# Warming matmuls, row sums, rotation copies and the last root in a one-core encoder block

## The chip, the cores and the metric

The kernel runs on one NeuronCore of a Trainium2 chip. The metric is the device time of one execution in microseconds, the median of several runs. Engines are called PE (TensorE matmul), PEld (its weight loads), DVE (VectorE), ACT (ScalarE), POOL (GpSimd) and SP (SyncE, which issues most transfers). PE writes to PSUM; ACT and DVE read it.

## The reference, cut to what matters

One layer over x of 512 rows and 1024 columns, all in float32:

```
h  = RMSNorm(x);  proj = h @ W_in          # q, k, v of differential attention; q, k, v, g of retention; two gates
dq, dk = rope(dq), rope(dk)
A  = differential attention (4 heads);  B = bidirectional retention (4 heads)
m  = sigmoid(gate_a) * (A @ W_upA) + sigmoid(gate_b) * (B @ W_upB)
x  = x + m @ W_o
x  = x + SwiGLU(RMSNorm(x))
y  = RMSNorm_final(x)
```

RMSNorm(x) is x * rsqrt(mean(x*x) + 1e-5) * g, with the mean along a row. rope turns pairs of columns of each head by an angle that depends on the row.

## The kernel before, in words

The work of all engines is written out by generators. Each generator yields the engine and the operands of its next instruction; `Streams.run` (L204) keeps a modelled clock for every engine and always emits the instruction that could start first by that model, with a rank to settle ties. The order of each engine's instructions is thus fixed at build time by modelled costs; on the chip every engine takes its list in order and waits only for data. A float32 matrix product is made of three products of float32r parts (`mm3`, L103): high by high, high by low, low by high. The splitting copies (`copy` on ACT, a subtraction on DVE) feed every product.

**Start.** `warm_gen` (L321) puts WARM = 9 matmuls of a 128x128 matrix of ones (float32, two records each in the trace) ahead of everything. Meanwhile `load_gen` (L335) fetches tiles of x and the first weights half by half; `conv_gen` (L386) splits the weights and `xsplit_gen` (L460) the x tiles, into `h_h` and `h_l`. `main_gen` (L1109) begins with the first four passes, "pfirst": four column tiles i of the projection (dq0, dk0, dq1, dk1), each a sum over eight tiles k of x, in a written order that follows what arrives: (0,0), (1,0), (0,1), (1,1), (2,0) and so on, the whole of tile 3 last. They sit in the PSUM pools "w" (three banks) and "o" (two banks).

**Row sums.** `xsquare_gen` adds up the squares of x, tile by tile. `rstd_gen` (L493) splits the sum, waits for the mark "pfirst" (set when all four passes are emitted), and lets PE sum over partitions: `ssq_b` (two matmuls of 512 columns) and `ssq_c` (four pairs of 4 columns, in a bank of the pool "mm", which has three). `rsqrt` (L480) makes the root: Ln, Exp and Square on ACT, then two `scalar_tensor_tensor` (STT) on DVE. It gives `rb`, with which the rope tables are scaled (`cosr` on DVE, `sinr` on POOL; then the mark "rope" is set), and `rcol`, a column for the values.

**Rotations.** `rope_gen` (L562), spawned for the four tiles after the passes, waits for "rope". Four ACT copies of 32 partitions swap quarters out of PSUM into `sw`; DVE makes `t1` = PSUM times `cosr` and the bank is released; POOL multiplies `sw` by `sinr` and adds it to `t1`; a split follows. `scores_gen` starts when q and k of a head are there. The later rotations (bank "mm") use the same function.

**Values.** `proj_v("dv")` (L1052) follows the passes: two groups of two row tiles, each group 48 matmuls. The second group can start only when two "mm" banks are free, so it waits for the evacuation of the first group's first tile (`v_evac_gen`, L721: ACT writes `dv_h` with the scale `rcol`, DVE writes `dv_l`).

**End.** The last stage adds the down projection to the residual and normalises row tile by row tile. `x2_gen` (L1001) adds PSUM to `x1t`, squares with a row sum (`accum_out`) into columns of `ss`, and multiplies by the gain into `u`. For the last tile, right half, add and square are done in two halves of 256 columns. `final_gen` (L1016) adds the columns of `ss` (a reduce), takes `rsqrt`, scales both halves of `u` (one on DVE, one on ACT for the last tile) and stores them.

Of the kernel before, what the change touches and what calls it, by code (L numbers as in the profile page):

```python
# [13 lines left out]
AF = mybir.ActivationFunctionType  # L14
ALU = mybir.AluOpType
AX = mybir.AxisListType

P = 128
T = 512
D = 1024  # L20
KT = D // P
NT = T // P
# [3 lines left out]
EPS = 1e-5  # L26
# [198 lines left out]
def block_kernel(ctx: ExitStack, tc: tile.TileContext, xT, w_st, w_v, w_g, w_up, w_o, w_f, w_fl,  # L225
# [8 lines left out]
    nc = tc.nc  # L234
# [7 lines left out]
    E = Streams(nc)  # L242
# [8 lines left out]
    done = set()  # L251

    def slot(name, dt=F32):
        return sp.tile([P, T], dt, tag="slot", name=name, bufs=NSLOT)
# [4 lines left out]
    def small(shape, name, dt=F32, bufs=1, tag=None):  # L259
        return cp.tile(shape, dt, tag=tag or name, name=name, bufs=bufs)  # L260

    def psum(tag, name):
        t = yield from E.acquire(tag)
        ps = pp.tile([P, T], F32, tag=tag, name=name, bufs=PS_BUFS[tag])
        E.mark(ps, t)
        return ps

    def split(src, name, after=None):

        h, l = slot(f"{name}_h", F32R), slot(f"{name}_l", F32R)  # L270
        yield from E.copy(h, src)
        yield from E.tt(l, src, h.bitcast(F32), ALU.subtract)
        return h, l

    def have(*names):
        return lambda: all(n in done for n in names)
# [22 lines left out]
            return (w_g if g[0] == "g" else w_db)[int(g[1]), b, u]  # L299
        return w_fl[b] if g == GROUPS - 1 else w_f[g, b, u]  # L300

    WARM = 9


    gcs = small([P, 25], "gcs")
# [6 lines left out]
    ones32 = small([P, P], "ones32")  # L312
# [3 lines left out]
    eps_c = small([P, 1], "eps_c")  # L316
# [4 lines left out]
    def warm_gen():  # L321

        ps = yield from psum("mm", "warm")
        for _ in range(WARM):
            nc.tensor.matmul(ps[:, 0:P], lhsT=ones32, rhs=ones32, start=True, stop=True)
        E.did("pe", 0.43 * WARM, [ps], [])
        E.release("mm", ps)

    xt, hh, hl = {}, {}, {}
# [125 lines left out]
    def drop(w):  # L455
        E.release("HL", w[1])
# [20 lines left out]
                yield from E.tt(acc, acc, sq, ALU.add)  # L477
        done.add("acc")

    def rsqrt(ps, n, name, out):  # L480

        w = ps.shape[-1]
        y0 = slot(f"{name}_y0")[:, :w]
        yield from E.act(out, ps, AF.Ln, scale=1.0 / n, bias=eps_c)
        yield from E.act(y0, out, AF.Exp, scale=-0.5)
        yield from E.act(out, y0, AF.Square, scale=math.sqrt(0.5 / n))
        yield from E.stt(out, ps, n * EPS, out, ALU.add, ALU.mult)
        yield from E.stt(out, out, 1.5, y0, ALU.subtract, ALU.mult, reverse0=True)

    rb, cosr, sinr = slot("rb"), slot("cosr"), slot("sinr")  # L490
# [2 lines left out]
    def rstd_gen():  # L493

        yield have("acc")
        ah, al = yield from split(acc, "accx")
        yield have("pfirst")
        ps = yield from psum("w", "ssq_b")
        yield from E.mm(ps, (ones, ah, True, False), (ones, al, False, True))
        ps2 = yield from psum("mm", "ssq_c")  # L500
        for j in range(NT):
            js = slice(j * P, (j + 1) * P)
            yield from E.mm(ps2[:, 4 * j:4 * j + 4], (ah[:, js], ones[:, 0:4], True, False),
                            (al[:, js], ones[:, 0:4], False, True))
        yield from rsqrt(ps, D, "rb", rb)
        E.release("w", ps)
        done.add("rb")
        yield from E.tt(cosr, cos_raw, rb, ALU.mult)
        yield from E.tt(sinr, sin_raw, rb, ALU.mult, eng="pool")
        done.add("rope")  # L510
        yield from rsqrt(ps2[:, 0:16], D, "rc", rcol)
        E.release("mm", ps2)
        done.add("rcol")
# [48 lines left out]
    def rope_gen(ps, bank, scale, name, key, is_k):  # L562

        yield have("rope")
        sw, t1 = slot(f"{name}_sw"), slot(f"{name}_t1")
        for a, b in ((0, 32), (32, 0), (64, 96), (96, 64)):
            yield from E.act(sw[a:a + 32, :], ps[b:b + 32, :], AF.Copy, scale=scale)
        yield from E.stt(t1, ps, scale, cosr, ALU.mult, ALU.mult)
        E.release(bank, ps)
        yield from E.tt(sw, sw, sinr, ALU.mult, eng="pool")  # L570
        yield from E.tt(t1, t1, sw, ALU.add, eng="pool")
        (ks if is_k else qs)[key] = yield from split(t1, name)

    def norm(po, name, gain=None, gate_tile=None):

        sq = slot(f"{name}_sq")
        yield from E.act(sq, po, AF.Square)
        sh, sl = yield from split(sq, f"{name}_sq")
        yield "pe", [sl]
        pn = yield from psum("w", f"{name}_ssq")  # L580
        yield from E.mm(pn, (ones, sh, True, False), (ones, sl, False, True))
        y = slot(f"{name}_y")
        yield from rsqrt(pn, P, name, y)
        E.release("w", pn)
        if gain is not None:
            yield from E.stt(y, po, gain, y, ALU.mult, ALU.mult)
            E.release("o", po)
        else:
            yield from E.tt(y, po, y, ALU.mult)
            E.release("o", po)  # L590
            yield have("rg")
            yield from E.tt(y, y, rg[gate_tile], ALU.mult, eng="pool")
        return (yield from split(y, f"{name}_o"))
# [407 lines left out]
    def x2_gen(i, hf, ps, ss):  # L1001

        t, u = x1t[i, hf], slot(f"u{i}{hf}")
        n = 2 if hf and i == NT - 1 else 1
        w = T // n
        for c in range(n):
            cs = slice(c * w, (c + 1) * w)
            yield from E.tt(t[:, cs], t[:, cs], ps[:, cs], ALU.add if i < 2 else ALU.subtract)
            sq = slot(f"sq3_{i}{hf}{c}")[:, :w]
            yield from E.act(sq, t[:, cs], AF.Square, accum_out=ss[:, hf + c:hf + c + 1])  # L1010
        yield from E.tt(u, t, gfs[hf], ALU.mult)
        X2[i, hf] = u

    X2 = {}

    def final_gen(i, ss):  # L1016
        yield lambda: (i, 0) in X2 and (i, 1) in X2
        s3, r3 = small([P, 1], f"s3_{i}"), small([P, 1], f"r3_{i}")
        yield from E.reduce(s3, ss, ALU.add)
        yield from rsqrt(s3, D, f"r3_{i}", r3)  # L1020
        a, b = X2[i, 0], X2[i, 1]
        yield from E.ts(b, b, r3, None, ALU.mult)
        yield from E.dma(y[i][:, T:D], b, sbuf_in=True)
        if i < NT - 1:
            yield from E.ts(a, a, r3, None, ALU.mult)
            yield from E.dma(y[i][:, 0:T], a, sbuf_in=True)
        else:
            yield from E.act(a, a, AF.Copy, scale=r3)
            yield from E.dma(y[i][:, 0:T], a, sbuf_in=True, q=nc.scalar)


    def proj_t(name, src, n_k=KT, w=None, off=0, bank="mm"):

        w0 = w or (yield from take())
        ps = yield from psum(bank, name)
        for k in range(n_k):
            cs = slice((off + k) * P, (off + k + 1) * P)
            yield lambda: k in src
            yield from E.mm3(ps, w0[0][:, cs], w0[1][:, cs], *src[k], k == 0, k == n_k - 1)
        if w is None:  # L1040
            drop(w0)
        return ps
# [66 lines left out]
    def main_gen():  # L1109
        ps0 = []  # L1110
# [4 lines left out]
        ws = {}  # L1115
        for i, k in order:
            yield lambda: ("conv", i, k // 4) in done and k in hh
            ws[i] = conv[i]
            cs = slice(k * P, (k + 1) * P)
            yield from E.mm3(ps0[i], ws[i][0][:, cs], ws[i][1][:, cs], hh[k], hl[k], k == 0, k == KT - 1)  # L1120
            if k == KT - 1:
                conv.pop(i)
                used[0] += 1
                drop(ws[i])
        done.add("pfirst")
        E.spawn(rope_gen(ps0[0], "w", 0.125, "dq0", 0, False), 10)
        E.spawn(rope_gen(ps0[1], "w", 1.0, "dk0", 0, True), 10)
        E.spawn(rope_gen(ps0[2], "o", 0.125, "dq1", 1, False), 11)
        E.spawn(rope_gen(ps0[3], "o", 1.0, "dk1", 1, True), 11)
        for h in range(HEADS):  # L1130
# [6 lines left out]
        for name in ORDER:  # L1137
# [4 lines left out]
            ps = yield from proj_t(name, hT)  # L1142
# [7 lines left out]
        for b, src in enumerate((oA, oB)):  # L1150
            for hf in range(2):
                us = []
                for i in range(NT):
                    ps = yield from psum("mm", f"up{hf}{b}{i}")
                    for k in range(HEADS):
# [3 lines left out]
                        cs, ts_ = slice(k % 2 * T, (k % 2 + 1) * T), slice(i * P, (i + 1) * P)  # L1159
# [24 lines left out]
        for n, ks_ in ((0, range(4)), (1, range(4)), (0, range(4, KT)), (1, range(4, KT)),  # L1184
# [4 lines left out]
            for k in ks_:  # L1189
                cs = slice(k * P, (k + 1) * P)  # L1190
# [24 lines left out]
        bank = {}  # L1215
# [30 lines left out]
        for i in range(NT):  # L1246
            ss = small([P, 3 if i == NT - 1 else 2], f"ss3_{i}")
            for hf in range(2):
                for k in range(FT - TAIL, FT):
                    yield from down(i, hf, k, k == FT - 1)  # L1250
                E.spawn(x2_gen(i, hf, pd[i, hf], ss), 10)
            E.spawn(final_gen(i, ss), 10)

    E.spawn(warm_gen(), 0)
    E.spawn(load_gen(), 0)
    E.spawn(conv_gen(), 2)
# [84 lines left out]
```

## Time and profile before

| | us |
|---|---|
| median of three runs | 725.46 (725.22 to 726.31) |
| the profiled execution | 725.72 |
| its span, first to last instruction | 723.5 |
| PE busy | 705.2 |
| DVE busy | 542.3 |
| ACT busy | 493.3 |

A timeline row is: start, duration, engine, line, operation, output <- inputs, shape, count, and in brackets the idle time just ahead and what ended it. A matmul's duration overlaps the next one's, so the pace of PE is read from one start to the next.

### The profile page before, as it was taken

The page shows a single profiled execution, that of the slowest core. Times are in us where ns is not written, and L with a number is a line of the kernel's source. Part 1 is how long each engine was busy: PE and PEld are TensorE (multiplying, and loading weights), DVE is VectorE, ACT ScalarE, POOL GpSimd, SP SyncE. Part 2 cuts the span into 40 slices and gives each one's busy share as a digit, 9 for nine tenths or more (in the row PEclk, how much of TensorE's full clock was granted, in tenths as well). Part 3 has the DMA queues.
Part 4 walks back from the last instruction along what each step waited for, and adds up shares of the span by engine and source line. Part 5 has one row for each costly group of instructions (what it writes and reads, how often), then busy time and mean ns, then how long its engine had stood idle before and what let it go on. Part 6 is the DMA issues. An engine that isn't in the chain of part 4 may idle for free.

```text
span 723.5 us, 9200 instructions
## 1 busy us (share of the span) xinstructions
PE 705.2 (97%) x3284; PEld 568.7 (79%) x3284; DVE 542.3 (75%) x796; ACT 493.3 (68%) x816; POOL 114.5 (16%) x137
## 2 busy tenths in 40 slices
PE   9989999999989999999999999999999999999996
PEld 7867677777758888887888888888888888787884
DVE  6667787869867478887677677667676789989645
ACT  7688897787687667665557876555656578777433
POOL 4360421011015001300000100000010011332000
PEclk9999999999999999999999999999999999999999
DMA  8802110302235628866522857658483887899202
GB/s 327 321 7 74 59 58 31 117 29 88 88 117 132 189 87 255 241 201 189 151 41 88 254 124 192 186 169 214 150 232 115 255 197 161 225 258 276 78 6 110
DMA packets 33661, 110.18 MB, mean 152 GB/s; under 512 B 4016, under 2 KB 4016, under 8 KB 33616
## 3 DMA queue, kind: packets, MB, share of 16 engines
q1 hardware_dynamic: 23328, 78.14, 30.7%
q0 software_dynamic: 10000, 30.94, 21.5%
q8 instruction: 25, 0.41, 0.2%
q10 hardware_dynamic: 288, 0.52, 0.2%
q14 instruction: 20, 0.16, 0.1%
HBM read 102.25 MB, written 2.10 MB: 144 GB/s over the span
## 4 chain that ended last, share of the span: by engine, by line
PE 84%; ACT 7%; DVE 6%; issue 1%; DMA 0%; SPq 0%; ACTq 0%; DVEq 0%
PE fY L91 16%; PE fZ L91 8%; PE wo L91 6%; PE up L91 6%; PE fYd L91 5%; PE fYg L91 5%; PE fX L91 4%; PE pfirst L91 3%; PE rg L91 3%; PE rv L91 3%; PE fZd L91 3%; PE fZg L91 3%; PE fXd L91 2%; PE dv L91 2%; PE fXg L91 2%; PE s L100 1%
## 5 line engine op out<-in xcount | busy, mean ns | idle before, releaser
L91 PE MATMUL fY<-w_h,S 128*128 128x512 f32 (+1 forms) x384 | 117.5, 376 | 0.0
L91 PEld LDWEIGHTS fY<-w_h,S 128*128 128x128 f32 x384 | 70.4, 188 | 12.1
L126 DVE TENSOR_TENSOR w_l<-w_r,w_h 128x1024 fp32r<-128x1024 f32 (+1 forms) x50 | 56.6, 1136 | 30.7 <-ACT w_h L121 30.2
L121 ACT CAST w_h<-w_r 128x1024 fp32r<-128x1024 f32 (+1 forms) x50 | 48.8, 980 | 34.6 <-issue 8.1
L91 PE MATMUL fY<-w_l,S 128*128 128x512 f32 (+1 forms) x192 | 71.4, 372 | 0.0
L91 PE MATMUL fZ<-w_h,S 128*128 128x512 f32 (+1 forms) x192 | 58.6, 377 | 0.0
L91 PE MATMUL fYd<-w_h,S 128*128 128x512 f32 x128 | 41.1, 391 | 0.0
L91 PEld LDWEIGHTS fY<-w_l,S 128*128 128x128 f32 x192 | 36.2, 189 | 5.7
L91 PEld LDWEIGHTS fZ<-w_h,S 128*128 128x128 f32 x192 | 35.3, 188 | 6.1
L91 PE MATMUL fZ<-w_l,S 128*128 128x512 f32 (+1 forms) x96 | 35.7, 371 | 0.0
L91 PE MATMUL fYg<-w_h,S 128*128 128x512 f32 x96 | 31.1, 391 | 0.0
L91 PE MATMUL fX<-w_h,S 128*128 128x512 f32 (+1 forms) x96 | 28.5, 371 | 0.0
L91 PEld LDWEIGHTS fYd<-w_h,S 128*128 128x128 f32 x128 | 24.0, 188 | 4.9
L116 ACT ACTIVATE fg<-fg,r 128x512 f32<-128x512 f32 (+1 forms) x24 | 16.0, 684 | 15.7 <-DVE fg L126 15.7
L91 PE MATMUL wo<-m_h,w_h 128*128 128x512 f32 x64 | 25.4, 397 | 0.0
L91 PE MATMUL wo<-m_l,w_h 128*128 128x512 f32 x64 | 25.1, 393 | 0.3 <-DVE m_l L126 0.2
L91 PE MATMUL wo<-m_h,w_l 128*128 128x512 f32 x64 | 24.9, 390 | 0.0
L91 PE MATMUL fYd<-w_l,S 128*128 128x512 f32 x64 | 24.9, 389 | 0.0
L169 POOL DMA_DIRECT2D x1t<-cd x20 | 18.0, 932 | 43.8 <-ACT cd L116 21.5
L150 DVE TENSOR_REDUCE mx<-s 128x1 f32<-128x512 f32 x32 | 21.2, 681 | 4.5 <-PE s L100 4.4
L116 ACT ACTIVATE e<-s,mx 128x512 f32<-128x512 f32 x32 | 21.9, 687 | 2.1 <-DVE mx L150 1.7
L121 ACT COPY snap_v<-fY 128x512 f32<-128x512 f32 (+1 forms) x24 | 13.2, 550 | 12.0 <-PE fY L91 12.0
(563 smaller groups left out, 2100.4 us busy)
## 6 DMA issues: line engine op xcount, KB each, us to landing
w_r<-w_st SPq DMA_DIRECT2D x12, 512.0 KB, 4.3
x1t<-cd POOLq DMA_DIRECT2D x20, 256.0 KB, 7.0
w_r<-w_v SPq DMA_DIRECT2D x8, 512.0 KB, 5.6
w_r<-w_up SPq DMA_DIRECT2D x8, 512.0 KB, 3.2
w_r<-w_o SPq DMA_DIRECT2D x8, 512.0 KB, 4.3
w_r<-w_d SPq DMA_DIRECT2D x6, 512.0 KB, 5.6
x<-xT SPq DMA_DIRECT2D x8, 256.0 KB, 5.6
w(g_a)_r<-w_g SPq DMA_DIRECT2D x4, 512.0 KB, 3.1
```

Of the source, the lines that this page charges most:

```text
L91: self.nc.tensor.matmul(out, lhsT=lhsT, rhs=rhs, start=start, stop=stop, skip_group_check=more)
L100: self.nc.tensor.matmul(outs[i % 2], lhsT=lhsT, rhs=rhs, start=i < 2, stop=i >= len(ops) - 2)
L116: self.nc.scalar.activation(out, in_, func, **kw)
L121: self.nc.scalar.copy(out=out, in_=in_)
L126: (self.nc.vector if eng == "dve" else self.nc.gpsimd).tensor_tensor(out=out, in0=a, in1=b, op=op)
L150: self.nc.vector.tensor_reduce(out=out, in_=a, axis=AX.X, op=op, **kw)
L169: self.nc.gpsimd.dma_start(out=out, in_=in_, accum_op=ALU.add)
```

## The change

- WARM is 10, and the warming generator adds one more matmul of ones after the mark "p0". That mark is set when the first three products of the passes, (0,0), are emitted; of these the low weight part now comes second and the low x part third.
- The mark "pfirst", on which the row sums wait, is set after (3,1) instead of after all passes.
- In rotations out of the pools "w" and "o" (the first four), the copies into partitions 0 to 63 are `tensor_scalar` on DVE; the other two stay on ACT.
- For the last row tile the sum of the first two columns of `ss` is formed on DVE as soon as they are there, and two scalars from it: sb = s/D + EPS (the bias of Ln) and sn = s + D*EPS (the addend of the first STT). The root then reads the third column of `ss` directly, without a reduce. The gain multiplication into `u` of the right half waits in the order for these three small instructions.

```
-    WARM = 9
+    WARM = 10
...
+        yield have("p0")
+        nc.tensor.matmul(ps[:, 0:P], lhsT=ones32, rhs=ones32, start=True, stop=True)
+        E.did("pe", 0.43, [ps], [])
...
-    def rsqrt(ps, n, name, out):
+    def rsqrt(ps, n, name, out, bias=None, more=None):
...
-        yield from E.act(out, ps, AF.Ln, scale=1.0 / n, bias=eps_c)
+        yield from E.act(out, ps, AF.Ln, scale=1.0 / n, bias=eps_c if bias is None else bias)
...
-        yield from E.stt(out, ps, n * EPS, out, ALU.add, ALU.mult)
+        yield from E.stt(out, ps, n * EPS if more is None else more, out, ALU.add, ALU.mult)
...
-            yield from E.act(sw[a:a + 32, :], ps[b:b + 32, :], AF.Copy, scale=scale)
+            if bank != "mm" and a < 64:
+                yield from E.ts(sw[a:a + 32, :], ps[b:b + 32, :], scale, None, ALU.mult)
+            else:
+                yield from E.act(sw[a:a + 32, :], ps[b:b + 32, :], AF.Copy, scale=scale)
...
+            if n == 2:
+                done.add(("ss3", "sq3")[c])
+        if n == 2:
+            yield have("ss3_n")
         yield from E.tt(u, t, gfs[hf], ALU.mult)
...
+            yield have("ss3")
+            sn, sb = small([P, 1], "s3_n"), small([P, 1], "s3_b")
+            yield from E.tt(s3, ss[:, 0:1], ss[:, 1:2], ALU.add)
+            yield from E.ts(sb, s3, 1.0 / D, EPS, ALU.mult, ALU.add)
+            yield from E.ts(sn, s3, D * EPS, None, ALU.add)
+            done.add("ss3_n")
+            yield lambda: (i, 0) in X2 and "sq3" in done
+            yield from rsqrt(ss[:, 2:3], D, f"r3_{i}", r3, sb, sn)
+            yield lambda: (i, 1) in X2
...
-            yield from E.mm3(ps0[i], ws[i][0][:, cs], ws[i][1][:, cs], hh[k], hl[k], k == 0, k == KT - 1)
+            wh, wl = ws[i][0][:, cs], ws[i][1][:, cs]
+            if (i, k) == (0, 0):
+                yield from E.mm(ps0[0], (wh, hh[0], True, False))
+                yield from E.mm(ps0[0], (wl, hh[0], False, False), (wh, hl[0], False, False))
+                done.add("p0")
+            else:
+                yield from E.mm3(ps0[i], wh, wl, hh[k], hl[k], k == 0, k == KT - 1)
+            if (i, k) == (3, 1):
+                done.add("pfirst")
...
-        done.add("pfirst")
```

## Rows read from the trace of the kernel before

**Rows 1.** The page's first part: busy time, share of the span, instructions.

```profile
PE 705.2 (97%) x3284; PEld 568.7 (79%) x3284; DVE 542.3 (75%) x796; ACT 493.3 (68%) x816; POOL 114.5 (16%) x137
```

**Rows 2.** Who waited for whom, PE alone: us in total, times, longest.

```profile
PE dv L91 <- DVE dv_l L132: 2.3, 1, 2.3
```

**Rows 3.** The timeline from the first matmul to 11 us.

```profile
0.98 4.21 PE L325 MATMUL warm<-ones 128*128 128x128 f32 x18 [0.98 <-POOL ones L313]
...
5.57 0.75 DVE L132 SCALAR_TENSOR_TENSOR h_l<-x,gcs,h_h 128x512 fp32r<-128x512 f32 x1 [0.31 <-ACT h_h L116]
...
5.58 0.80 PE L91 MATMUL pfirst<-h_h,w_h 128*128 128x512 f32 x1 [0.40 <-ACT h_h L116]
...
6.62 0.62 ACT L121 CAST w_h<-w_r 128x512 fp32r<-128x512 f32 x1 [1.09 <-DMA w_r<-w_st]
...
8.36 0.75 DVE L132 SCALAR_TENSOR_TENSOR h_l<-x,gcs,h_h 128x512 fp32r<-128x512 f32 x1 [0.31 <-ACT h_h L116]
...
9.75 0.63 PE L91 MATMUL pfirst<-h_h,w_l 128*128 128x512 f32 x1
...
10.18 0.48 PE L91 MATMUL pfirst<-h_h,w_h 128*128 128x512 f32 x1
...
10.50 0.39 PE L91 MATMUL pfirst<-h_l,w_h 128*128 128x512 f32 x1
...
10.73 0.40 PE L91 MATMUL pfirst<-h_h,w_l 128*128 128x512 f32 x1
```

**Rows 4.** Passes and row sums: the chain that ended last (start, us, what), then timeline rows.

```profile
5.58 24.62 PE pfirst L91 x96
...
22.64 0.69 DVE L126 TENSOR_TENSOR accx_l<-acc_x,accx_h 128x512 fp32r<-128x512 f32 x1
...
30.04 0.39 PE L91 MATMUL ssq_b<-accx_h,ones 128*128 128x512 f32 x1
...
31.00 0.68 ACT L116 ACTIVATE rb<-ssq_b,eps_c 128x512 f32<-128x512 f32 x1
...
33.78 0.69 DVE L132 SCALAR_TENSOR_TENSOR rb<-rb,rb_y 128x512 f32<-128x512 f32 x1
...
33.87 0.59 ACT L116 ACTIVATE dq_sw<-pfirst 32x512 f32<-32x512 f32 x1
```

**Rows 5.** The timeline around the start of the second group of dv.

```profile
42.78 0.39 PE L91 MATMUL dv<-w_h,h_l 128*128 128x512 f32 x1
45.47 0.50 PE L91 MATMUL dv<-w_h,h_h 128*128 128x512 f32 x1 [2.29 <-DVE dv_l L132]
...
43.82 0.69 ACT L116 ACTIVATE dv_h<-dv,rcol 128x512 fp32r<-128x512 f32 x1
...
43.22 1.53 DVE L126 TENSOR_TENSOR dq_l<-dq_t,dq_h 128x512 fp32r<-128x512 f32 x1
44.67 0.74 DVE L132 SCALAR_TENSOR_TENSOR dv_l<-dv,rcol,dv_h 128x512 fp32r<-128x512 f32 x1
```

**Rows 6.** Busy time by stretch: length, PE, PEld, DVE, ACT, POOL, granted clock, DMA.

```profile
30.20:43.00 12.80, 12.80 (x62) 10.50 (x60) 5.99 (x9) 11.92 (x22) 6.96 (x6) 1.00 0.25 93
...
80.00:106.00 26.00, 24.11 (x112) 17.34 (x112) 19.66 (x34) 23.40 (x44) 7.34 (x6) 1.00 0.14 45
```

**Rows 7.** DVE's groups between 28 and 50 us, by form: busy, mean ns, idle before.

```profile
L132 DVE SCALAR_TENSOR_TENSOR dq_t<-pfirst,cosr 128x512 f32<-128x512 f32 x2 | 1.4, 692 | 3.3 <-ACT dq_sw L116 3.3
```

**Rows 8.** The timeline after the last matmul.

```profile
717.15 0.19 ACT L116 ACTIVATION_READ_ACCUMULATOR sq<-x1t 128x1 f32 x1
717.16 0.69 DVE L126 TENSOR_TENSOR u<-x1t,gf 128x512 f32<-128x512 f32 x1
...
717.55 0.18 ACT L116 ACTIVATION_READ_ACCUMULATOR sq<-x1t 128x1 f32 x1
717.77 0.15 DVE L150 TENSOR_REDUCE s<-ss 128x1 f32<-128x3 f32 x1
717.96 0.30 ACT L116 ACTIVATE r<-s,eps_c 128x1 f32<-128x1 f32 x1 [0.22 <-DVE s L150]
...
718.52 0.20 ACT L116 ACTIVATE r<-r_y 128x1 f32<-128x1 f32 x1
718.75 0.16 DVE L132 SCALAR_TENSOR_TENSOR r<-s,r 128x1 f32<-128x1 f32 x1 [0.83 <-ACT r L116]
```

More of the change, by code (lines that the diff above doesn't have):

```diff
@@ L1016, in final_gen @@
     def final_gen(i, ss):
-        yield lambda: (i, 0) in X2 and (i, 1) in X2
         s3, r3 = small([P, 1], f"s3_{i}"), small([P, 1], f"r3_{i}")
-        yield from E.reduce(s3, ss, ALU.add)
-        yield from rsqrt(s3, D, f"r3_{i}", r3)
+        if i < NT - 1:
+            yield lambda: (i, 0) in X2 and (i, 1) in X2
+            yield from E.reduce(s3, ss, ALU.add)
+            yield from rsqrt(s3, D, f"r3_{i}", r3)
+        else:
[8 more added lines that the diff above has]
+            yield lambda: (i, 1) in X2
         a, b = X2[i, 0], X2[i, 1]
@@ L1119, in main_gen @@
             cs = slice(k * P, (k + 1) * P)
-            yield from E.mm3(ps0[i], ws[i][0][:, cs], ws[i][1][:, cs], hh[k], hl[k], k == 0, k == KT - 1)
+            wh, wl = ws[i][0][:, cs], ws[i][1][:, cs]
[3 more added lines that the diff above has]
+                done.add("p0")
+            else:
+                yield from E.mm3(ps0[i], wh, wl, hh[k], hl[k], k == 0, k == KT - 1)
+            if (i, k) == (3, 1):
+                done.add("pfirst")
             if k == KT - 1:
```

## The prediction, made before the run

> **What bounds the kernel now.** The page's busy shares come first: PE is busy 97% of the span [rows 1], so time can come only from stretches in which PE stands still or runs slowly, and from the two ends. Three views show them. The waits of PE alone: the longest in the middle is one wait of 2.3 us of the values' second group on DVE's `dv_l` [rows 2]. The timeline of the start: PE's pace there is half of the later one [rows 3]. The timeline of the end: after the last matmul one chain through DVE and ACT [rows 8]. ACT and DVE are not the bound over the span, but in the stretch from 30.2 to 43.0 us ACT is busy 11.92 of 12.80 us and DVE 5.99 [rows 6]. So the question is what the end of the passes hands to these two engines, and when.
>
> **Start.** Nine warming matmuls take 4.21 us from 0.98, to 5.19; PE then idles until the first pass at 5.58 [rows 3]. From 9.75 to 10.18 one matmul of 512 columns passes in 0.43 us, which is the 1.2 GHz level; from 10.50 to 10.73 in 0.23, the 2.4 GHz level (as later, where the granted clock is 1.00 [rows 6]), though PE had been given work from 0.98 on, with holes. A tenth warming matmul (4.21 / 9 = 0.47) ends at about 5.66, so the first hole closes and the first pass is 0.08 late. Its second product now uses the low weight part; the low part of x is there at 5.57 + 0.75 = 6.32 [rows 3], before the third product at 5.66 + 2 x 0.43 = 6.52. The second hole closes too, and (0,0) ends at 6.95. The added matmul (0.47 at the slow level) runs to 7.42, against weights for (1,0) that come at 6.62 + 0.62 = 7.24: at most 0.2 late, and absorbed, because (0,1) waits anyway for `h_l` of the second x tile, 8.36 + 0.75 = 9.11 [rows 3]. If the clock is up by then, its second and third product start at 9.17 and 9.40, (1,1) at 9.62 and its second product at 9.85, against 10.50: 0.65 us won. Ends: 0.65, all that the arrival of x allows, and -0.1, if the clock rises no sooner and something of the added matmul shows. I take 0.65, since the row nearest to unbroken work is the one after which the pace doubles.
>
> The Trainium skill, TensorE: Matmul & The Clock Gate, "What's actually happening", says that the default state is throttled and activity releases it, and that the moment isn't tied to the kernel's start and varies from run to run. By that rule some executions of before rise early already and the gain on the median is less; one trace can't show it.
>
> **Row sums.** The passes take 24.62 us for 32 steps [rows 4]; the last six steps are 6 x 3 x 0.227 = 4.1 us. The split sum is ready at 22.64 + 0.69 = 23.33, so `ssq_b` can follow (3,1) at about 30.04 - 4.1 - 0.65 = 25.3. The matmuls are the same ones, moved: PE's sum doesn't change. What changes is the root: Ln at 31.00 to the last STT at 33.78 + 0.69 = 34.47 [rows 4] now lies beside the passes, from about 26.2 to 29.7, and `cosr` and `sinr` behind it. The rotations, whose first ACT copy stood at 33.87, start when the passes end: 30.20 - 0.65 + 0.9 for the row sums now in front of that end = 30.5. That is 3.4 us earlier.
>
> **Shared copies.** Sixteen ACT copies of 0.59 [rows 4] become eight on each engine. ACT sheds 4.7 us of its 11.92, and the root's three operations besides. A DVE copy out of PSUM of 32x512 is not in the trace: from below ACT's 0.59, from above DVE's 0.69 for 512 elements with one operand in PSUM [rows 7]; I take 0.65, nearer to the row on the same engine, so DVE gains 5.2 us and loses the root's 1.4. Added to 5.99 that is 9.8 of 12.8, so DVE still has room, if splits and scores that now come early don't fill it. No transfer is added or moved; SP's and POOL's queues keep their order around this, and POOL's two multiplications a rotation start as much earlier as the copies do.
>
> **The stall of dv.** The second group starts at 45.47, when `dv_l` ends (44.67 + 0.74 = 45.41); the last matmul ahead of it started at 42.78 [rows 5]. At full pace the next would have started at 43.01, so 2.46 us are lost. `dv_h` started at 43.82 behind copies on ACT and `dv_l` behind `dq_l`, which took 1.53 on DVE [rows 5]. With both engines free, what is left is the way itself: the first tile's last matmul is three matmuls (0.68) ahead of 42.78, so starts at 42.10; it drains in 0.39, `dv_h` takes 0.69, `dv_l` 0.74, and three hand-overs some 0.04 each: 44.04, a loss of 1.03. Ends of the loss: 0, if scores, whose q and k come some 6 us earlier (3.4, and four of eight copies of 0.59 gone from ACT), fill the hole; and above the old 2.46, if DVE is late. I take 1.03: gain 1.43. Late next is that same evacuation.
>
> The order of the queues matters here. `dq_l` reads two SBUF tensors and stood still beside a POOL multiplication, 1.53 instead of about 0.69 [rows 5]. The Trainium skill, SBUF — State Buffer, "SBUF: two separate sides", calls this an exclusive lock: a DVE operation with two SBUF inputs and a POOL one shut each other out for the whole instruction. By it the new copies, which read PSUM, cost nothing extra, but the earlier splits still can.
>
> **End.** The reduce waits for the second row sum (717.55 + 0.18 = 717.73) and Ln starts at 717.96 [rows 8]. Afterwards the sum of the first two columns can start at 717.15 + 0.19 + 0.04 = 717.38; two dependent small DVE steps of 0.15 to 0.20 put sb at 717.72, and Ln starts at 717.77 behind ACT's own read: 0.19 earlier. The delayed `u` (0.69) begins behind sn at about 717.8 and ends at 718.5, just as Square ends at 718.72 - 0.19 = 718.53, so it is covered by a hair. Ends: +0.19, and -0.2 if the first sum has to wait for the second read (717.77, then two hops: Ln at 718.16). I take 0.19, since the columns are separate. Final scaling and transfers follow unchanged.
>
> **Sum.** 0.65 + 1.43 + 0.19 = 2.27 us. The profiled execution took 725.72, 2.2 of it outside its span of 723.5; that part stays, and the sum makes it 723.45. It lies 0.26 above the median; taken from the median, 725.46 - 2.27 = 723.2, which I forecast.
>
> **Rivals.** One: more than the sum. The scores' chain leads by several us, fills the dv hole (1.03 more) and takes half of the 1.89 us that PE idles from 80 to 106 us, where ACT is busy 23.40 of 26.00 [rows 6]: about 721.2. For it: ACT and DVE get work earlier, in a time in which DVE was half idle. Against: the order is written by a model, and any change of modelled times reshuffles what follows.
>
> Two: the stall stays, DVE taking ACT's place. Then only the ends remain: 725.46 - 0.84 = 724.6. For it: the 1.53 of `dq_l` [rows 5].
>
> Three, slower: DVE's list between 30 and 43 us overflows. Its 5.99 less 1.4 plus eight copies at 0.69 (5.5), plus two splits of 1.53 [rows 5] and two of 0.69 [rows 4] brought forward and two maxima out of PSUM at 0.69 [rows 7] are 15.9 us in 12.8, and `dv_l` lies behind all of it: 3.1 late, a stall of 4.1, minus 0.84 at the ends: 726.3. It decides from a stall above 3.3 us; with one more stretched split (0.84) each on `dv_h`'s release and on the weights' low parts it is 728.
>
> Four: the change at the start does nothing (the rise of the clock lies where it lay): 723.2 + 0.65 = 723.9.
>
> **Chances.** Forecast 0.42, rival one 0.22, two 0.17, three 0.10, four 0.09. The measurement of this kernel can tell about 0.2%, 1.45 us. Below 724.0 lie the forecast, rival one and part of four: 0.68. Rival two, the rest of four, and three's milder part: 0.26. Slower: 0.06. The range goes from 720.6 (rival one with the whole 1.89 and a little) to 725.2 (rival two with the start's gain gone).
>
> **What would show it.** Right: 512-column starts 0.23 apart before 9.4 us; `ssq_b` near 25.4 us, and the first rotation copy near 30.5; PE's wait on `dv_l` near 0.9 us; Ln straight behind the last accumulator read. Wrong: a pace of 0.43 still at 9.7; a wait on `dv_l` of 2 us or more with DVE busy throughout; PE waits after 80 us that sum to more than before, which would be the reshuffled order.

## The result, and the profile after

The changed kernel took 721.43 us (median of six executions, the lowest 720.82), the kernel before beside it 725.34 (six, 724.2 to 726.31): a ratio of 0.9947 (0.9932 to 0.9962), 3.9 us or 0.53% faster, more than the 0.2% that can be told apart. The forecast was 723.2 with a range of 720.6 to 725.2: right in sign and in range, but 1.8 us short of the gain.

One of the six, the execution first profiled, ran at a mean granted clock of 0.655 and took 1000.94 us, unlike any other here: that median counts it (the other five have a median of 720.90 and a mean of 721.49), the ratio leaves it out, and its rows aren't used. The rows of after are those of the last run below, where the same file was profiled again: 720.81 us, span 719.0, granted clock 0.998.

The page's first part, after:

```profile
PE 703.2 (98%) x3288; PEld 568.9 (79%) x3288; DVE 549.4 (76%) x806; ACT 488.2 (68%) x808; POOL 114.0 (16%) x137
```

PE has four instructions more than in [rows 1] and is still the bound. ACT sheds 5.1 us of work, DVE takes 7.1. Who waited for whom, PE alone (us in total, times, longest):

```profile
PE ro L91 <- DVE an_y L132: 1.9, 1, 1.9
PE at L109 <- ACT e L116: 1.5, 1, 1.5
PE aT L109 <- DVE fa L132: 1.3, 1, 1.3
PE fZd L91 <- DVE w_l L132: 1.2, 2, 0.8
```

The 2.3 us on `dv_l` [rows 2] are gone from the list, not smaller. The timeline around the start of the second group of dv shows what stands there instead:

```profile
40.25 0.39 PE L91 MATMUL dv<-w_h,h_l 128*128 128x512 f32 x1
...
40.68 1.37 ACT L116 ACTIVATE dv_h<-dv,rcol 128x512 fp32r<-128x512 f32 x2
...
40.93 0.39 PE L91 MATMUL dv<-w_h,h_l 128*128 128x512 f32 x1
...
41.25 0.50 PE L100 MATMUL s<-dk_h,dq_h 64*128 64x512 f32 x2
...
41.40 0.75 DVE L132 SCALAR_TENSOR_TENSOR dv_l<-dv,rcol,dv_h 128x512 fp32r<-128x512 f32 x1
...
42.16 0.50 PE L91 MATMUL dv<-w_h,h_h 128*128 128x512 f32 x1
```

One group of scores runs on PE from 41.25 to about 42.1, while `dv_l` is made; it ends at 41.40 + 0.75 = 42.15 and the next product starts at 42.16. (The 40.25 is the last matmul of the first tile, on which the evacuation waits.) Against [rows 5] the evacuation ends 3.3 us earlier, and only about 0.1 us of PE is lost where 2.46 were.

Why it ends earlier, from the row sums to the rotations, all engines:

```profile
24.73 0.39 PE L91 MATMUL ssq_b<-accx_h,ones 128*128 128x512 f32 x1
...
25.46 0.69 ACT L116 ACTIVATE rb<-ssq_b,eps_c 128x512 f32<-128x512 f32 x1 [0.33 <-PE ssq_b L91]
...
28.23 0.69 DVE L132 SCALAR_TENSOR_TENSOR rb<-rb,rb_y 128x512 f32<-128x512 f32 x1
...
29.76 0.68 DVE L139 TENSOR_SCALAR dq_sw<-pfirst 32x512 f32<-32x512 f32 x1
...
31.58 1.20 ACT L116 ACTIVATE dq_sw<-pfirst 32x512 f32<-32x512 f32 x2 [0.29 <-DVE dq_sw L139]
...
34.86 1.20 ACT L116 ACTIVATE dk_sw<-pfirst 32x512 f32<-32x512 f32 x2 [2.08 <-DVE dk_sw L139]
```

The root ends at 28.92, beside the passes, instead of 34.47, and the first rotation copy stands at 29.76 instead of 33.87 [rows 4]. In the last two rows ACT waits for DVE's copies into the same tile. Busy time by stretch (length, PE, PEld, DVE, ACT, POOL, granted clock, DMA), as in [rows 6]:

```profile
30.20:43.00 12.80, 12.80 (x59) 10.08 (x59) 12.28 (x19) 8.31 (x13) 9.59 (x8) 1.00 0.19 72
80.00:106.00 26.00, 23.95 (x112) 18.15 (x112) 21.03 (x37) 23.51 (x43) 7.70 (x6) 1.00 0.19 61
```

ACT fell from 11.92 to 8.31, but DVE rose from 5.99 to 12.28 of 12.80: nothing is left of its room. From 80 to 106 us nothing was won.

The start, PE alone, and the tail, all engines:

```profile
0.98 4.63 PE L325 MATMUL warm<-ones 128*128 128x128 f32 x20 [0.98 <-POOL ones L313]
5.73 0.80 PE L91 MATMUL pfirst<-h_h,w_h 128*128 128x512 f32 x1
6.32 0.47 PE L91 MATMUL pfirst<-h_h,w_l 128*128 128x512 f32 x1
6.63 0.39 PE L91 MATMUL pfirst<-h_l,w_h 128*128 128x512 f32 x1
6.86 0.38 PE L328 MATMUL warm<-ones 128*128 128x128 f32 x2
...
8.50 0.50 PE L91 MATMUL pfirst<-h_l,w_h 128*128 128x512 f32 x1 [0.29 <-DVE h_l L132]
```

```profile
711.57 0.39 PE L91 MATMUL pd<-w_h,act_l 128*128 128x512 f32 x1
...
712.99 0.16 DVE L126 TENSOR_TENSOR s<-ss 128x1 f32<-128x1 f32 x1 [0.24 <-ACT sq L116]
713.17 0.19 ACT L116 ACTIVATION_READ_ACCUMULATOR sq<-x1t 128x1 f32 x1
...
713.32 0.68 DVE L126 TENSOR_TENSOR u<-x1t,gf 128x512 f32<-128x512 f32 x1
713.43 0.29 ACT L116 ACTIVATE r<-ss,s_b 128x1 f32<-128x1 f32 x1
...
714.23 0.22 DVE L132 SCALAR_TENSOR_TENSOR r<-ss,s_n,r 128x1 f32<-128x1 f32 x1 [0.23 <-ACT r L116]
...
714.68 0.72 ACT L116 ACTIVATE u<-u,r 128x512 f32<-128x512 f32 x1 [0.48 <-DVE r L132]
```

The 2.4 GHz pace is there from 6.63 on (the next instruction follows 0.23 later) instead of 10.50 [rows 3]. Here it is read from the pace, because the profile's granted clock says 1.00 throughout the start, also from 9 to 10 us in the trace of before, where the pace is 0.43. PE then waits ahead of 8.50 for the second x tile. In the tail Ln starts right behind the accumulator read.

Where the 4.5 us between the two spans (723.5 and 719.0) lie: the first product of the two branch gates (`fYg`) stands at 254.00 before and at 250.03 after, so 3.97 us are won ahead of it, 0.40 on the long way behind it, and 0.09 in the tail (last matmul to final scaling: 715.94 to 719.14 before, 711.57 to 714.68 after). Of the 3.97, 2.36 are the hole of dv (2.46 - 0.1) and 1.07 the start and passes: dv begins at 30.27 instead of 30.65, and before three pairs of row sums at 0.23 still followed. Some 0.5 is spread over the rest.

### The profile page after: what moved, and what is told of

Its sections match the earlier page's. It is cut to its first block, busy times and chain, and to the rows that moved or that the text cites. A ratio compares the mean times of both kernels' runs of the same rounds, so it can differ in the third digit from the quotient of the medians.

```text
span 999.2 us, 9206 instructions
## 1 busy us (share of the span) xinstructions
PE 989.4 (99%) x3288; PEld 639.4 (64%) x3288; DVE 558.1 (56%) x806; ACT 495.4 (50%) x808; POOL 113.0 (11%) x137
## 4 chain that ended last, share of the span: by engine, by line
PE 97%; DMA 1%; DVE 1%; ACT 0%; SPq 0%; issue 0%
PE fY L91 17%; PE fZ L91 9%; PE fYd L91 7%; PE fYg L91 6%; PE wo L91 6%; PE up L91 6%; PE fX L91 4%; PE fZd L91 4%; PE rv L91 3%; PE dv L91 3%; PE fZg L91 3%; PE pfirst L91 3%; PE rg L91 3%; PE fXd L91 3%; PE s L100 2%; PE dq L91 2%
## 5 line engine op out<-in xcount | busy, mean ns | idle before, releaser
L91 PE MATMUL fY<-w_h,S 128*128 128x512 f32 (+1 forms) x384 | 157.0, 484 | 0.0
L91 PEld LDWEIGHTS fY<-w_h,S 128*128 128x128 f32 x384 | 80.1, 215 | 36.3 <-issue 11.3
L91 PE MATMUL fY<-w_l,S 128*128 128x512 f32 (+1 forms) x192 | 91.9, 479 | 0.0
L91 PE MATMUL fZ<-w_h,S 128*128 128x512 f32 (+1 forms) x192 | 78.6, 487 | 0.0
L91 PE MATMUL fYd<-w_h,S 128*128 128x512 f32 x128 | 55.4, 508 | 0.0
L91 PE MATMUL fZ<-w_l,S 128*128 128x512 f32 (+1 forms) x96 | 46.0, 479 | 0.0
L91 PE MATMUL fYg<-w_h,S 128*128 128x512 f32 x96 | 41.5, 509 | 0.0
L91 PE MATMUL fX<-w_h,S 128*128 128x512 f32 (+1 forms) x96 | 38.3, 479 | 0.0
L91 PE MATMUL fZd<-w_h,S 128*128 128x512 f32 x64 | 27.5, 507 | 0.0
L91 PEld LDWEIGHTS fYg<-w_h,S 128*128 128x128 f32 x96 | 20.0, 208 | 11.1 <-issue 3.5
```

What stands on the lines that cost most here:

```text
L91: self.nc.tensor.matmul(out, lhsT=lhsT, rhs=rhs, start=start, stop=stop, skip_group_check=more)
```

## The experiments

Ratios are to the kernel before, measured beside the runs: its median is 725.67 us for the whole change and the three parts taken out or back, 726.11 for each part alone, the filled hole of dv and the first filling of the late hole, 725.58 for the two by-tile runs and the last two. A ratio is formed from all executions and need not be the quotient of the medians. None leaves out a part of the computation; "filling" matmuls multiply ones into a bank that nothing reads.

**The whole change, and each part taken out or back.** First the change itself, with no edit:

> The whole change, for an undisturbed profile. Theory A (the sum, plus the later stalls of rival one): clock up before 9.4 us, PE's wait ahead of the second dv group at or below 1.0 us instead of 2.3, and the 1.6 us by which the median fell more than the sum found as smaller PE waits between 80 and 212 us. Theory B (the front stages give it all): the dv wait gone altogether, another 1.0 us, and the passes over 1 us shorter, with the waits after 80 us as before. Time 721.0 to 722.0.

Measured: 721.81 us, 0.9951 (0.9938 to 0.9963).

Without the warming:

```diff
-    WARM = 10
+    WARM = 9
-        yield have("p0")
-        nc.tensor.matmul(ps[:, 0:P], lhsT=ones32, rhs=ones32, start=True, stop=True)
...
-            if (i, k) == (0, 0):
...
+            yield from E.mm3(ps0[i], wh, wl, hh[k], hl[k], k == 0, k == KT - 1)
```

> The change with WARM = 9, no added matmul and the old order of the first three products. Theory A: 0.65 us slower than the whole change, about 722.0, with a pace of 0.43 us to about 10 us. Rival (the clock rises when it likes): the same time as the whole change within 0.2 us on the median.

Measured: 722.21 us, 0.9954 (0.9941 to 0.9967), 0.4 above the whole, with overlapping intervals. Its timeline of the start, PE alone:

```profile
9.67 0.63 PE L91 MATMUL pfirst<-h_h,w_l 128*128 128x512 f32 x1
...
10.45 0.39 PE L91 MATMUL pfirst<-h_l,w_h 128*128 128x512 f32 x1
10.67 0.40 PE L91 MATMUL pfirst<-h_h,w_l 128*128 128x512 f32 x1
```

In this execution the clock rises where it rose before. But four of the six profiled executions here with nine warming matmuls (this one, the kernel before, and four further runs below) rose by 6.3 us, and all seven with ten by 7.0. That the tenth makes an early rise regular fits these counts but is not shown by them, and what it is worth on the median lies below what these runs tell apart.

The row sums' mark behind the passes again, the rest of the change kept:

```diff
-            if (i, k) == (3, 1):
+            if (i, k) == (3, KT - 1):
                 done.add("pfirst")
```

> The change with the mark of the row sums after all passes, as before. Theory A: the rotations start 3.4 us later again, but with copies on two engines the dv wait stays below the old 2.3: about 1.2 to 1.6 us, so 0.3 to 0.6 us slower than the whole change, and more if the later waits come back. Rival (the early root is the whole gain of this stage): dv wait 2.3 again, 1.5 to 2.5 us slower.

Measured: 736.16 us, 1.0148 (1.0134 to 1.0162): slower than the kernel before by 10.5 us. PE's longest wait, and two stretches (columns as above):

```profile
PE dv L91 <- DVE dv_l L132: 3.5, 1, 3.5
```

```profile
45.00:50.00 5.00, 3.51 (x8) 2.82 (x9) 5.00 (x5) 1.25 (x3) 4.75 (x4) 0.51 0.01 2
91.50:94.50 3.00, 0.83 (x4) 0.32 (x3) 2.96 (x4) 0.62 (x1) 1.35 (x2) 1.00 0.01 3
```

The wait on `dv_l` grew from 2.29 to 3.5 us with DVE busy 5.00 of 5.00, and behind it the granted clock is 0.51, the 1.2 GHz level. This is the slower rival. Both expectations missed it: neither had a wait longer than that of the kernel before.

The shared copies all on ACT again:

```diff
-            if bank != "mm" and a < 64:
+            if False:
                 yield from E.ts(sw[a:a + 32, :], ps[b:b + 32, :], scale, None, ALU.mult)
```

> The change with all sixteen first copies on ACT. Theory A: the root is early, the copies run from 30.5 to about 40 us on ACT alone, in time for dv's first evacuation at 42 us: dv wait about 1.0, time within 0.4 us of the whole change. Rival (the sharing is what empties ACT in time): dv wait 1.5 to 2.3 and 0.5 to 1.3 us slower.

Measured: 721.88 us, 0.9953 (0.9941 to 0.9965), the whole's time. With early row sums the sharing is worth nothing that can be told.

**One part alone, on the kernel before.** The early mark alone (`done.add("pfirst")` behind (3, 1) in place of behind the passes):

> The kernel before with the mark of the row sums after (3,1), nothing else. Theory A (the early root alone empties ACT and DVE in time): PE's wait on dv_l gone or below 0.3 us, 722.3 to 722.9, the rest to the whole change being the warming and the root. Rival (the early sums need the shared copies): a wait of 1 us or more and 724 or above.

Measured: 722.45 us, 0.9947 (0.9928 to 0.9966). One moved line gives the gain of the whole change, as near as these intervals can tell. The sharing alone:

```diff
-            yield from E.act(sw[a:a + 32, :], ps[b:b + 32, :], AF.Copy, scale=scale)
+            if bank != "mm" and a < 64:
+                yield from E.ts(sw[a:a + 32, :], ps[b:b + 32, :], scale, None, ALU.mult)
+            else:
+                yield from E.act(sw[a:a + 32, :], ps[b:b + 32, :], AF.Copy, scale=scale)
```

> The kernel before with the first rotations' copies shared with DVE, nothing else. Theory A (DVE is late when the root has not been moved; the hole then costs the clock): PE's wait on dv_l 3.3 us or more, a stretch at the 1.2 GHz level behind it, 734 to 737. Rival (the slow time of the third run came from the warming and the sharing together): within 1 us of the kernel before.

Measured: 736.76 us, 1.0147 (1.0127 to 1.0167). PE's longest wait, and the stretch behind it:

```profile
PE dv L91 <- DVE dv_l L132: 3.6, 1, 3.6
```

```profile
45.00:48.50 3.50, 2.83 (x7) 2.25 (x8) 3.50 (x4) 0.68 (x2) 3.42 (x3) 0.52 0.01 2
```

The same as with late sums in the whole: the wait is 1.3 us longer than before, and the clock falls here and, in this run, again at 92.9 to 96.3 and 215.8 to 222.6 us. At half speed these 13.7 us cost at most 6.9 of the 10.7 lost. PE also stands still more: from 60 to 270 us it idles 10.8 us here and 9.5 with late sums in the whole, where the kernel before has 4.3. The planner's order of the attention stage is another one too: behind the hole twelve matmuls of dv come ahead of the first scores, where the kernel before has three. What that order costs by itself, no run separates.

**Is it the shared tile, or DVE's load?** In the run above ACT's first copies of `dq_sw` and `dk_sw` waited 2.8 and 1.6 us for DVE's. One theory: two engines that write one tile hold each other up. The other: DVE has too much. So whole tiles went to either engine, `k` to DVE and `q` to ACT, with as many copies on each:

```diff
-            if bank != "mm" and a < 64:
+            if bank != "mm" and is_k:
```

> The sixth run's kernel (sharing alone), but each rotation's four copies on one engine: the two q tiles on ACT, the two k tiles on DVE, eight copies each as there. Theory A (in the sixth run ACT's two copies of a tile wait for DVE's two of the same tile, so the sharing is a queue through both engines): ACT's waits on DVE's copies are gone, PE's wait on dv_l 1.0 to 2.3 us, clock 1.00 behind it, 723 to 727. Rival B (DVE has too much to do, whoever waits): the wait stays above 3.3 us, 734 to 737. Rival C (the order of the attention stage that this planning gives is bad by itself): a short wait on dv_l, but the later holes and the clock's falls behind them remain: 730 to 735.

Measured: 739.83 us, 1.0196 (1.0181 to 1.0211), worse than any of the three expectations. ACT's copies, DVE's evacuation, and PE behind it:

```profile
34.41 3.61 ACT L116 ACTIVATE dq_sw<-pfirst 32x512 f32<-32x512 f32 x6
...
40.83 0.69 ACT L116 ACTIVATE dv_h<-dv,rcol 128x512 fp32r<-128x512 f32 x1 [1.17 <-PE dv L91]
...
44.44 1.40 DVE L139 TENSOR_SCALAR dk_sw<-pfirst 32x512 f32<-32x512 f32 x2
45.87 0.69 DVE L132 SCALAR_TENSOR_TENSOR dk_t<-pfirst,cosr 128x512 f32<-128x512 f32 x1
46.47 1.25 DVE L126 TENSOR_TENSOR dq_l<-dq_t,dq_h 128x512 fp32r<-128x512 f32 x1
47.65 1.40 DVE L132 SCALAR_TENSOR_TENSOR dv_l<-dv,rcol,dv_h 128x512 fp32r<-128x512 f32 x2
...
48.44 0.79 PE L91 MATMUL dv<-w_h,h_h 128*128 128x512 f32 x1 [6.29 <-DVE dv_l L132]
```

ACT's waits for DVE are gone, six copies run on end, and yet PE's wait grew to 6.3 us: DVE works without a gap at copies, a rotation and a split that stand ahead of `dv_l` in its list. `dv_h` is done at 40.83 + 0.69 = 41.52, so it isn't what `dv_l` waits for until 47.65; it is its place in DVE's list. The first theory fell; the second is what the rows show, with the order of the list as much as its length. The same edit in the whole change, with the filling of the late hole described next:

> The whole change with the copies shared by tile as in the ninth run, and the late hole filled as in the eighth. Theory A: nothing is left to win at the passes' end (the dv wait is gone already), so the same as the eighth run within 0.3 us, 721.2 to 721.7, and no execution with a mean clock below 0.997. Rival (earlier rotations bring the attention stage forward): 0.5 us less.

Measured: 723.82 us, 0.998 (0.997 to 0.999), where 721.2 to 721.7 was expected: 1.7 us behind the whole beside it (722.12) and 2.4 behind the whole with the late hole filled (721.46, below). The `k` tiles came late, as PE's waits say:

```profile
PE s L100 <- DVE dk_l L126: 1.6, 1, 1.6
```

**What does a hole cost through the clock?** To the late-sums kernel, 14 matmuls of ones were added in the hole of dv, with the order otherwise the same:

```diff
+            if (name, g, k, i) == ("dv", 1, 0, 1):
+                fill = yield from psum("w", "fill")
+                for _ in range(14):
+                    nc.tensor.matmul(fill[:, 0:P], lhsT=ones32, rhs=ones32, start=True, stop=True)
```

> The third run's kernel with 14 matmuls of ones (128x128, float32) put between the two first dv products of the second group, in the hole in which PE waits on dv_l; every other instruction and its order is the same. Theory A (PE standing still is what lets the clock fall): granted clock 1.00 from 43 to 55 us, dv at 0.23 a matmul, 3.0 to 3.5 us less than the third run, so 732.6 to 733.2. Rival (the clock falls for another reason): still at the 1.2 GHz level there, and 0 to 0.3 us slower than the third run.

Measured: 735.29 us, 1.0125 (1.0105 to 1.0145), 0.9 us below the unfilled one (1.7 by the ratios, whose intervals overlap): less than the 2.9 us that PE leads by behind the hole, and less than the 3.0 to 3.5 expected. The filling, and the two stretches shown above for the unfilled one:

```profile
42.43 3.29 PE L1089 MATMUL fill<-ones 128*128 128x128 f32 x28
...
46.11 0.50 PE L91 MATMUL dv<-w_h,h_h 128*128 128x512 f32 x1 [0.39 <-DVE dv_l L132]
```

```profile
45.00:50.00 5.00, 4.61 (x26) 3.26 (x24) 5.00 (x6) 2.66 (x4) 4.40 (x3) 1.00 0.02 5
91.50:94.50 3.00, 3.00 (x10) 1.49 (x10) 0.88 (x2) 0.00 (x0) 0.00 (x0) 0.50 0.00 0
```

The clock stays at 1.00 behind the filled hole, so the hole did bring it down. But the lead (first `ao` product at 83.77 instead of 86.64) is mostly given back: the next hole, 2.2 us on `aT_l`, is not smaller, and now the clock falls behind it, at 91.5, where the unfilled kernel, still in its own hole there, then went on at 1.00. So filling the hole of dv shows what brings the clock down, but not that the clock makes up most of the 10.5 us that late sums lose: with it held up there, 9.2 are still lost, part of them to its falls behind later holes.

The whole change has such a hole too: 1.9 us in front of the last retention head, in its list of waits. In its first profile here (722.46 us) the clock fell behind it: the product that ended it, and the stretch after.

```profile
204.74 0.77 PE L91 MATMUL ro<-rd_h,rv_h 128*128 128x512 f32 x1 [1.91 <-DVE an_y L132]
```

```profile
205.00:208.00 3.00, 3.00 (x8) 2.32 (x9) 0.69 (x1) 2.94 (x5) 2.38 (x4) 0.50 0.16 60
```

So eight matmuls of ones went into that hole of the whole change, the rest of the order unchanged:

```diff
+        if (h, j) == (HEADS - 1, 0):
+            fill = yield from psum("w", "fill")
+            yield "pe", [po, *sT[h, j]]
+            for _ in range(8):
+                nc.tensor.matmul(fill[:, 0:P], lhsT=ones32, rhs=ones32, start=True, stop=True)
```

> The whole change with 8 matmuls of ones put ahead of the last retention head's first product, in the hole of 1.9 us near 203 us; every other instruction and its order is the same. Theory A (part of the executions loses some 1.6 us to a clock that falls behind that hole): no execution above 721.8, mean clock 0.997 or 0.998 in all, median 720.8 to 721.1. Rival (the fall has another cause, or the filling delays the product): the same mix of 720.8 and 722.5, or 0.2 to 0.5 us more.

Measured: 721.46 us, 0.9934 (0.9918 to 0.9950), all six executions between 720.92 and 721.65. The same stretch:

```profile
205.00:208.00 3.00, 3.00 (x13) 2.52 (x14) 0.48 (x1) 2.96 (x5) 2.65 (x4) 1.00 0.35 64
```

The same filling on the early mark alone:

> The kernel before with the early row sums and the late hole filled, without added warming, sharing or the shorter root. Theory A (the early sums are nearly all of the gain): within 0.6 us of the tenth and the twelfth run's undisturbed executions, 721.0 to 721.9, the clock's rise at the start differing from run to run. Rival (the other three parts carry over 1 us): 722.2 or more.

Measured: 721.18 us, 0.9944 (0.9932 to 0.9955), beside the unedited change:

> The whole change again, beside the two filled kernels on one chip. Theory A: a mix of executions near 720.9 and 722.5, the later ones with a mean clock of 0.995 or 0.996, median 0.2 to 0.8 us above the tenth run's. Rival (the filling doesn't matter): equal medians within 0.2 us.

Measured: 722.12 us, 0.9953 (0.9941 to 0.9966); in its profile the clock stays at 1.00 behind the same hole of 1.9 us:

```profile
205.00:208.00 3.00, 3.00 (x15) 2.33 (x14) 0.69 (x1) 2.94 (x5) 2.27 (x3) 1.00 0.20 51
```

So the hole is always there and the fall is not: in three more profiles above (without the warming, copies on ACT, early mark alone) the hole is 1.9 us too, and the clock stays at 1.00 behind it. Over the 17 executions of the change with a usable clock, 7 have a mean granted clock of 0.996 or less and took 722.37 to 723.26 us, 10 have 0.997 or more and took 720.75 to 721.96. Of the 11 of the two filled kernels that carry the early sums as written (the whole change and the mark alone), all have 0.997 or more and took 720.71 to 722.04. (The by-tile run, filled too, has four of eight at 0.994 or 0.995; none of these was profiled, so where its clock fell is open.) That the fall in the profiled execution stands for all seven is inferred from their means; only profiled ones show the place. On the average the filling brought little: the 11 have a mean of 721.37, the 17 of 721.79, and the 10 of these whose clock stayed up of 721.11. The early mark with the filled hole (721.18) is as good as the whole change (722.12 beside it) by the least edit; their intervals overlap.

## Why the prediction came out as it did

**Start, 0.65 forecast.** The course is as forecast: the pace doubles by 6.63, sooner than said, and dv starts earlier. That the tenth matmul is the cause isn't shown, and the size isn't either. Some executions of nine matmuls rise early as well, 4 of 6 profiles by 6.3 us, the two others past 10.3. The Trainium skill, TensorE: Matmul & The Clock Gate, "What's actually happening", says that the moment varies from run to run. The traces agree, with these counts; the prediction had it as the alternative. Moreover x lands when it lands, and the sum took its landing as fixed. The second x tile's `h_l` was ready at 9.11 in the trace of before [rows 3] and at 7.69 + 0.75 = 8.44 in that of after, so up to 0.67 of the 1.07 us at the passes may be the landing's. Over the eight profiles with early sums dv begins between 30.3 and 31.4 us, and 31.4 is the start both without the warming (pace doubled at 10.45) and in the profile of the early mark with the filled hole, where the pace was up by 6.64 and PE then waited for the second x tile until 9.63. On the median, with against without was 0.4 us, undecided.

**Row sums, 3.4 us earlier.** Right in kind: `ssq_b` at 24.73 (25.3 forecast), the root over at 28.92 (29.7), the first copy at 29.76 (30.5), a lead of 4.1. It didn't wait for the end of the passes, as the prediction had it: the last matmul of these starts at 30.04.

**Shared copies.** 0.68 us each on DVE, forecast 0.65 between 0.59 and 0.69. But "DVE still has room" failed: 12.28 of 12.80 us, since splits and scores that came early filled it. The early sums pay for it, starting DVE's list earlier; without them the list ends late, as the two runs at 1.0148 and 1.0147 show. The prediction counted the sharing as part of what shortens the stall. It isn't: left out, the time stays.

**The dv stall, 1.43 forecast.** This is the term that was mis-sized. The way itself was right: from the first tile's last matmul to the end of `dv_l` it takes 42.15 - 40.25 = 1.90 us, where 1.94 was said, although DVE is busy nearly throughout. But of the loss of 1.03 only about 0.1 was measured, because one group of scores (0.9 us) lies in the hole. The prediction named that as the lower end, 0, and as rival one, with 0.22. By the rows it should have been the forecast: scores' q and k were said to come 6 us earlier, and the order is written by a planner that has them ready. Corrected, the sum is 0.65 + 2.36 + 0.19 = 3.2, and the median from 725.46 would be 722.3.

**End, 0.19 forecast, 0.09 measured.** All eight profiles with the shorter root have 3.11 or 3.12 us from the last matmul to the final scaling, all five with the old one 3.19 or 3.20, so this small gain is shown. Ln starts 0.16 earlier after the last matmul (2.02 us before, 1.86 after). Part goes back: the first step of the root on DVE now takes its scalar from a tensor and lasts 0.22 us, where its counterpart lasts 0.16 [rows 8]. The `u` that was delayed is covered, as said: it ends at 714.00, before DVE's first step of the root at 714.23.

**The rivals.** One happened by half: the dv hole filled, but from 80 to 106 us PE idles 2.05 us where it idled 1.89, and the later stalls merely have other places. Two and four did not happen, except that nine matmuls also can rise early. Three is real, once the sums are late: its price was 726.3 to 728, while late sums gave 736.2. The stall was near its sum (3.5 of 4.1). What it lacked was all that follows the stall: the clock, which falls behind it and behind later ones, and the 9.5 us that PE idles from 60 to 270 us. The range's lower end was mis-added: rival one with the whole 1.89 is 723.2 - 1.03 - 1.89 = 720.3, not 720.6.

**The rest of the gain.** 3.9 measured against the corrected 3.2. Part of the difference may be which executions are compared. The kernel before has executions with a lower mean clock as well, and more of them: of its 36 executions beside the experiments, 24 have 0.996 or less (mean 725.97 us) and 12 have 0.997 or more (724.81); the change has 7 (722.76) and 10 (721.11) of 17. Like against like, the gain is 3.2 and 3.7 us. Where the clock of the kernel before falls is open, since its profile is one in which it didn't. The landing of x differs between profiled executions too, and some 0.5 us is spread between 43 and 254 us; no run separates these.

## What to carry to other kernels

When a stall has a producer with two loaded engines ahead of it, first ask what can be made *earlier* (here one mark, moved six steps forward); moving work from the one to the other was worth nothing here once the producer was early, and harmful while it was late. When a stall shrinks, cost what becomes ready to fill it, by the planner's own rule, before taking the bare latency as what remains. Look behind each long hole of PE for the granted clock: a fall behind a hole of 1.9 us went with about 1.7 us more here. Idle matmuls in the hole kept the clock up, but the lead that they buy can be waited away at the next one.

## What was not expected of the hardware

The granted clock fell from 1.00 to 0.50 or 0.52 behind holes of PE of 1.9 us in some executions and not in others (0.50 in one profile of the change, 1.00 in another, with the same order and the same hole), and behind all three holes of 3.5 to 6.3 us at dv; behind the 2.29 us at dv in the trace of before it stayed at 1.00. In the profile that fell, PE had been busy 22.80 of 22.80 us at 1.00 from 180 us to that hole. Matmuls of ones in the hole, whose results go nowhere, kept it at 1.00 in the profiles.

DVE's copy of 32 partitions by 512 elements out of PSUM takes 0.68 us, as long as its operations on 128 partitions out of PSUM (0.69). And a copy on ACT waited for a copy on DVE into other partitions of the same tile: 2.08 us in the rows above; by-tile sharing took the wait away. The copies themselves kept their time (0.60 us each on ACT), and the profile infers such a wait from a semaphore; both speak for the program's dependences, but it was not tried.
